# Attention scores of a streaming encoder: two matmuls of 128 and 64 rows per head become three of 64 rows, with two heads on two row groups in turn

## The chip, the cores and the metric

The kernel runs on one core of one Trainium2 chip. The metric is device time in microseconds, lower is better. Times are the median of several executions; the profile is one further execution, recorded by the hardware profiler, in which TensorE is called PE, its weight load PEld, VectorE DVE, ScalarE ACT, GpSimd POOL and the queue engine SP.

## The reference, cut to what matters

The program is one layer of a hybrid encoder: a gated linear recurrence (HGRN2) on half of the width, chunk-band attention on the other half, then an output product and a squared-ReLU MLP. It runs for a prompt of 2048 tokens and for eight streams of 16 tokens. Only the attention of the prompt is touched here. For each of 8 heads of width 64:

```
rel  = clip(kpos[None, :] - qpos[:, None], -128, 128) + 128
s    = q k^T * (1 / sqrt(64)) + rel_bias[:, rel]     # float32
s    = where(key in the chunk band, s, -1e30)
o    = softmax(s) v
```

A query of chunk c (64 tokens) reads the keys of the chunks c-8 to c. All inputs are float32, and the products are wanted at about float32 accuracy.

## The kernel before, in words

**Splitting for accuracy.** Nearly all products are made from matmuls of the type fp32r, which keeps fewer bits than fp32. So an operand x is kept as a high part, x rounded to fp32r, and a low part, the rest; a product is then hi·hi + hi·lo + lo·hi, three matmuls (`mm3`, lines 290 to 292). Weights are split while they stream in: ACT makes `whi` (line 256), DVE makes `wlo` (line 257).

**Stages.** Three stages follow one another: HGRN (up to about 783 us of the profile), attention (783 to 1484 us), MLP (from 1484 us). In the attention stage two streams of work are written out side by side by `weave`: `att_proj` (products for q, k, v of each group of up to three token tiles of 128, and the output product two groups behind), and `att` (the attention itself). The scheduler of the language then orders each engine's instructions; an engine runs its instructions strictly in that order. So the products of the first stream (`mm<-...`, 256 or 384 columns wide) are the filler that PE has while the softmax of a tile is worked on by DVE and ACT.

**One step of the attention** (`att_group`) is one token tile and one feature tile `ft`, that is, two heads e = 0 and 1: 16 tiles x 4 feature tiles, 64 steps. In each step:

1. PE makes the scores `S` of both heads (lines 679 and 680), 128 queries x up to 640 keys. With five key tiles (12 of the 16 token tiles) the 640 columns are made in two halves of 320; with fewer, in one piece of 128 to 512 columns. Each head has an `S` of two PSUM banks of its own.
2. DVE adds the bias and takes the minimum (`s<-S,bias`, line 688), ACT takes the exponential (`s<-s,m`, line 690), head by head.
3. PE transposes the probabilities of each head (`S<-ident,s`, line 699), back into the same PSUM; DVE copies one head's and ACT the other's to `pt` (line 700).
4. PE multiplies with v (`ps_oT<-pt,vt`, line 706). The two heads use 64 columns of the array each, in turn.

**The scores before.** Line 679 is a matmul over all 128 rows of the array: q's high part of head e stands twice, in the rows of e and in the other 64 rows (`q[:, e, :]`), and `K[:, e, :]` has k's high part in the rows of e and its low part in the other rows; so one matmul gives hi·hi + hi·lo. Line 680 adds lo·hi from 64 rows alone. Head e = 1 follows when e = 0 is complete:

```
nc.tensor.matmul(S[:, bk, :n], q[:, e, qc], c.K[ft][:, e, kc], start=True, stop=False)
nc.tensor.matmul(S[:, bk, :n], ql[es, qc], c.K[ft][es, e, kc], start=False, stop=True)
```

To lay the parts out in this way, `att_proj_group` takes for each feature tile of q four ACT instructions of 64 partitions (lines 881 and 885, once for each head) and two of DVE (line 882), and for each feature tile of k two of ACT (line 912) and two of DVE (line 913).

Of the kernel before, what the change touches and what calls it, by code (L numbers as in the profile page):

```python
# [8 lines left out]
F32 = mybir.dt.float32  # L9
F32R = mybir.dt.float32r  # L10
# [7 lines left out]
P = 128  # L18
D = 1024
KT = D // P  # L20
NPT = 16            # token tiles of the prompt; tile 16 holds the 8x16 sample tokens
NTT = 17
# [4 lines left out]
BIG = 1e30  # L27
WC = 256            # weight columns taken at a time

# [42 lines left out]
def rsq(c, ss, n, width, key="", r=None):  # L72
    """(ss / width + eps) ** -0.5 for a [P, n] tile of sums of squares"""
    nc = c.nc
    if r is None:
        r = c.small.tile([P, 8], F32, tag="r" + key, name="r", bufs=4)
    nc.gpsimd.tensor_scalar(out=r[:, :n], in0=ss, scalar1=1.0 / width, scalar2=EPS,
                            op0=ALU.mult, op1=ALU.add)
    nc.gpsimd.tensor_tensor(out=r[:, :n], in0=r[:, :n], in1=c.mhalf[:, :n], op=ALU.pow)
    return r  # L80
# [14 lines left out]
def transpose_split(c, src, hi, lo, col, nk=KT):  # L95
    """token rows src [P, nk*128] -> feature-major hi/lo parts [P, nk, col:col+128]"""
    nc = c.nc
    for k0 in range(0, nk, 4):
        ps = c.ps_tx.tile([P, 4, P], F32, tag=c.ps_tx_tag, name="tx")
        for k in range(4):  # L100
            nc.tensor.transpose(ps[:, k, :], src[:, (k0 + k) * P:(k0 + k + 1) * P], c.ident)  # L101
        h = hi[:, k0:k0 + 4, col:col + P]
        nc.scalar.copy(h, ps)
        nc.vector.tensor_tensor(out=lo[:, k0:k0 + 4, col:col + P], in0=ps, in1=h.bitcast(F32),  # L104
                                op=ALU.subtract)


def norm_rows(c, x, g, out, key=""):
    """out = x * rsqrt(mean(x^2) + eps) * g"""
    r = rsq(c, sumsq(c, x, D, key), 1, D, key)  # L110
    c.nc.vector.scalar_tensor_tensor(out=out, in0=x, scalar=r[:, 0:1], in1=g,
                                     op0=ALU.mult, op1=ALU.mult)


def weave(a, na, b, nb):
    """emit two streams of work side by side; a stream yields the share of work that it has emitted,
    or None while it waits for another"""
    done = [0.0, 0.0]
    live = [True, True]
    turn = None  # L120
    idle = 0
    while any(live):
        i = turn if turn is not None else int(done[0] * nb > done[1] * na)
        turn = None
        if not live[i]:
            i = 1 - i
        try:
            w = next((a, b)[i])
        except StopIteration:
            live[i] = False  # L130
            continue
        if w is None:
            turn = 1 - i
            idle += 1
            if idle > 1 or not live[1 - i]:
                yield None
                idle = 0
        else:
            done[i] += w
            idle = 0  # L140
            yield w
# [7 lines left out]
class HT:  # L149
    """normalised tokens of a group, feature-major, as hi/lo parts"""  # L150

# [7 lines left out]
    def pre(self, n=1):  # L159
        """loads of the next n token tiles"""  # L160
        while n and len(self.ld) < len(self.tiles) and self.ready():
# [3 lines left out]
    def add(self):  # L165
        """the next token tile"""
        j = self.next
# [37 lines left out]
def token_scale(c, t):  # L205
    """rsqrt of the mean square of the tokens of a tile, kept as a row of the scratch too"""
    nc = c.nc
# [7 lines left out]
class OT(HT):  # L215
    """mixer outputs of a group, feature-major, as hi/lo parts"""

# [24 lines left out]
class W:  # L242
    """a block [P, (nk, ncol)] of a weight matrix as hi/lo parts, in pieces"""

# [22 lines left out]
def wseq(c):  # L267
    """all blocks of weights in the order of their use, each prepared while the one before is in use"""
    srcs = [(c.w_in[i], WC) for _ in GROUPS for i in (4, 2, 3, 0, 1, 5, 6, 7)]
# [15 lines left out]
def mm3(c, ps, pairs, parts=1):  # L285
    """ps = sum of lhsT^T rhs over (lh, ll, rh, rl) parts, three passes each; yields between the parts"""
    nc = c.nc
# [13 lines left out]
def proj_fm(c, w, hT, n, parts=PARTS):  # L301
    """feature-major products, one PSUM tile after the other: yields (feature tile, columns, PSUM),
    before that as often as parts say without PSUM"""
    hi, lo = hT.hi, hT.lo
# [10 lines left out]
def proj_tm(c, w, hT, js, parts=PARTS):  # L315
    """token-major products: yields (token tile, PSUM) likewise"""
    hi, lo = hT.hi, hT.lo
# [15 lines left out]

# ---------------------------------------------------------------- HGRN

def lower_bound(c, pool):
    """lb = cumsum(softmax(lb_param, 0), 0) - softmax(lb_param, 0)[0], feature-major [P, 4]"""
    nc = c.nc
# [15 lines left out]
def hgrn_proj(c, gs, start):  # L354
    """projections of all groups, one after the other"""
    nc = c.nc
# [80 lines left out]
def hgrn_tile(c, g, j, t, seq):  # L437
    """one tile of 128 tokens: products of f between tokens, built up by doubling blocks"""
    nc = c.nc
# [122 lines left out]
def phase_hgrn(c):  # L562
    tc, nc = c.tc, c.nc
    with ExitStack() as s:
# [36 lines left out]
        def turn(act):  # L601
            """a level of each tile under way, until the first is done"""
            while True:
# [29 lines left out]

# ---------------------------------------------------------------- attention

def att_bias(c, h0, n):
    """negated bias of n heads, with the chunks that a row must not read"""
    nc = c.nc
# [7 lines left out]
def att_finish(c, o, t):  # L646
    """o [P, 512] token-major, normalised over its 512 features, to the scratch"""
    nc = c.nc
# [5 lines left out]
def att_group(c, g, tiles):  # L654
    """attention of a group's prompt tiles, one feature tile (two heads) after the other"""
    nc = c.nc
# [3 lines left out]
    for ft in range(4):  # L660
# [4 lines left out]
        for j, i in enumerate(tiles):  # L665
# [6 lines left out]
            st = []  # L672
            for e in range(2):
                h = 2 * ft + e
                es = slice(64 * e, 64 * e + 64)
                S = c.ps_s.tile([P, 2, 512], F32, tag="S", name="S")
                for (bk, o, n) in halves:
                    kc = slice(k0 + o, k0 + o + n)
                    nc.tensor.matmul(S[:, bk, :n], q[:, e, qc], c.K[ft][:, e, kc], start=True, stop=False)  # L679
                    nc.tensor.matmul(S[:, bk, :n], ql[es, qc], c.K[ft][es, e, kc], start=False, stop=True)  # L680
                s = c.sp.tile([P, 640], F32, tag="s", name="s")
# [45 lines left out]
def att_sample(c, qbd, kraw, vs):  # L727
    """8 streams x 16 queries over 256 cached and 16 new keys"""
    nc = c.nc
# [59 lines left out]
def att_proj(c, gs):  # L789
    """q, k, v of all groups and, two groups behind, w_out"""  # L790
    todo = TODO
# [19 lines left out]
def out_group(c, oT, nxt, pool=None):  # L811
    """x + [o_h, o_a] w_out, to the scratch"""
    nc = c.nc
# [26 lines left out]
def att_v(c, vt, tiles, hT):  # L840
    """the first half of v, by way of the tiles that hold all of it"""
    for t in tiles:
# [11 lines left out]
def att_proj_group(c, gs, gi, vt, hT, nxt):  # L854
# [13 lines left out]
    for ch in range(2):  # L868
        w = next(c.ws)
        for f, cs, ps in proj_fm(c, w, hT, n):  # L870
# [3 lines left out]
            ft = ch * 2 + f  # L874
            q = c.qp_.tile([P, 2, GMAX], F32R, tag="qd", name="qd")
            ql = c.qp_.tile([P, GMAX], F32R, tag="ql", name="ql")
            g.q[ft] = (q, ql)
            for e in range(2):
                src = slice(64 * e, 64 * e + 64)
                oth = slice(64 - 64 * e, 128 - 64 * e)  # L880
                nc.scalar.activation(q[src, e, :npr], ps[src, :npr], AF.Copy, scale=-0.125)
                nc.vector.scalar_tensor_tensor(
                    out=ql[src, :npr], in0=ps[src, :npr], scalar=-0.125,
                    in1=q.bitcast(F32)[src, e, :npr], op0=ALU.mult, op1=ALU.subtract)
                nc.scalar.activation(q[oth, e, :npr], ps[src, :npr], AF.Copy, scale=-0.125)
            if sample:
# [4 lines left out]
    for ch in range(2):  # L891
        w = next(c.ws)
        for f, cs, ps in proj_fm(c, w, hT, n):
# [14 lines left out]
            kc = slice(512, 512 + npr)  # L908
            for e in range(2):
                src = slice(64 * e, 64 * e + 64)  # L910
                oth = slice(64 - 64 * e, 128 - 64 * e)
                nc.scalar.copy(K[src, e, kc], raw[src, :npr])
                nc.vector.tensor_tensor(out=K[oth, e, kc], in0=raw[src, :npr],
                                        in1=K.bitcast(F32)[src, e, kc], op=ALU.subtract)
            fs = slice(ft * P, (ft + 1) * P)
# [59 lines left out]

# ---------------------------------------------------------------- MLP

# [22 lines left out]
def sample_mixer(c):  # L1000
    """attention and w_out of the sample tokens"""
    tc, nc = c.tc, c.nc
# [211 lines left out]
```

## Time and profile before

| | |
|---|---|
| median of 3 runs | 3121.32 us (3119.15 to 3126.25) |
| profiled execution, span from first to last instruction | 3136.9 us |
| PE busy | 2996.8 us (96%) |
| PE's weight loads | 2728.8 us (87%) |
| DVE busy | 1778.4 us (57%) |
| ACT busy | 1154.7 us (37%) |
| POOL busy | 302.5 us (10%) |
| DMA moved | 330.45 MB, mean 105 GB/s |

For the profiled execution nothing but its span is given, so the span stands for its time; it is 15.6 us longer than the median of the runs. Busy times of PE are modelled: a matmul's record covers its passage through the pipeline, so records that follow each other overlap, and what a matmul costs is read from the distance between the starts of two, not from the length of one.

### The profile page before, as it was taken

The numbers are of one execution on the slowest core, as the hardware profiler recorded it, in microseconds if no ns is written. First come the engines' busy times: TensorE is split into PE (matmuls) and PEld (weight loads), VectorE is DVE, ScalarE is ACT, GpSimd is POOL, SyncE is SP. The second block draws the span as 40 slices with busy tenths as digits, with TensorE's granted clock in tenths as the row PEclk, the third lists the DMA queues.
The fourth block names the chain that finished last, engine by engine and source line by source line (L and its number), as shares of the span: only waits on it lengthen the run. The fifth ranks groups of instructions, "written<-read, shape, count | busy, mean of one in ns | idle before, by whom it ended". The sixth has DMA issues, their size and how long they took to land.

```text
span 3136.9 us, 46880 instructions
## 1 busy us (share of the span) xinstructions
PE 2996.8 (96%) x18678; PEld 2728.8 (87%) x18678; DVE 1778.4 (57%) x3162; ACT 1154.7 (37%) x2354; POOL 302.5 (10%) x509
## 2 busy tenths in 40 slices
PE   5689999998999999999899999999999999999998
PEld 5678999998878888888888899999999999899997
DVE  3347566775546555565555545556555555655555
ACT  3332334344654545454422332323222222332332
POOL 2221222221002010100200000001000000000000
PEclk8789999999999999999999999999999999999999
DMA  8764233344315132333832232214221221422222
GB/s 156 154 123 130 92 124 111 105 136 135 109 55 165 64 127 84 130 127 123 287 101 81 83 111 93 88 61 155 68 68 60 67 67 56 147 70 79 81 71 71
DMA packets 118795, 330.45 MB, mean 105 GB/s; under 512 B 14192, under 2 KB 42480, under 8 KB 118576
## 3 DMA queue, kind: packets, MB, share of 16 engines
q1 hardware_dynamic: 111712, 308.84, 33.0%
q0 software_dynamic: 6864, 18.63, 1.5%
q8 instruction: 146, 2.39, 0.3%
q14 instruction: 73, 0.60, 0.1%
HBM read 294.90 MB, written 32.51 MB: 104 GB/s over the span
## 4 chain that ended last, share of the span: by engine, by line
PE 84%; DMA 8%; DVE 3%; issue 2%; POOL 2%; ACT 1%; SPq 0%; ACTq 0%; POOLq 0%; DVEq 0%
PE mm L290 23%; PE mm L292 23%; PE mm L291 23%; DMA x<-in_x_prompt 3%; PE ps_oT L706 2%; PE S L680 2%; PE S L679 2%; PE S L699 2%; PE ps_sc L472 2%; DMA wraw<-in_w_in 1%; DMA rd<-r 1%; DVE wlo L257 1%; DMA xT<-in_x_T 1%; PE tx L101 1%; PE ps_sc L465 1%
## 5 line engine op out<-in xcount | busy, mean ns | idle before, releaser
L256 ACT CAST whi<-wraw 128x512 fp32r<-128x512 f32 x816 | 498.0, 620 | 748.9 <-PE mm L292 550.4
L257 DVE TENSOR_TENSOR wlo<-wraw,whi 128x512 fp32r<-128x512 f32 x816 | 563.5, 707 | 245.0 <-ACT whi L256 241.1
L290 PE MATMUL mm<-h_hi,whi 128*128 128x384 f32 (+1 forms) x1536 | 503.6, 328 | 0.0
L292 PE MATMUL mm<-h_hi,wlo 128*128 128x384 f32 (+1 forms) x1536 | 502.0, 327 | 0.0
L291 PE MATMUL mm<-h_lo,whi 128*128 128x384 f32 (+1 forms) x1536 | 501.5, 326 | 0.0
L1087 DVE TENSOR_TENSOR y<-mm,y 128x512 f32<-128x512 f32 x544 | 373.7, 689 | 221.6 <-PE mm L292 219.9
L290 PE MATMUL mm<-whi,hT_hi 128*128 128x256 f32 x1264 | 385.7, 305 | 43.9 <-DVE gate L382 20.0
L292 PE MATMUL mm<-whi,ul 128*128 128x512 f32 x1088 | 424.1, 390 | 0.0
L291 PE MATMUL mm<-wlo,uh 128*128 128x512 f32 x1088 | 424.0, 390 | 0.0
L290 PE MATMUL mm<-whi,uh 128*128 128x512 f32 x1088 | 423.5, 389 | 0.0
L292 PE MATMUL mm<-whi,hT_lo 128*128 128x256 f32 x1264 | 375.5, 297 | 4.9 <-DVE hT_lo L104 3.5
L291 PE MATMUL mm<-wlo,hT_hi 128*128 128x256 f32 x1264 | 374.1, 296 | 0.0
L290 PEld LDWEIGHTS mm<-whi,hT_hi 128*128 128x128 f32 x1264 | 254.7, 202 | 56.0 <-DVE gate L382 21.2
L290 PEld LDWEIGHTS mm<-h_hi,whi 128*128 128x128 f32 x1536 | 289.0, 188 | 4.2 <-issue 2.6
L290 PE MATMUL mm<-hT_hi,whi 128*128 128x384 f32 (+1 forms) x768 | 266.3, 347 | 26.3 <-ACT sig L401 17.2
L291 PEld LDWEIGHTS mm<-h_lo,whi 128*128 128x128 f32 x1536 | 288.9, 188 | 1.2
L292 PEld LDWEIGHTS mm<-h_hi,wlo 128*128 128x128 f32 x1536 | 288.9, 188 | 0.0
L292 PEld LDWEIGHTS mm<-whi,hT_lo 128*128 128x128 f32 x1264 | 255.2, 202 | 9.8 <-DVE hT_lo L104 4.8
L1065 DVE SCALAR_TENSOR_TENSOR u<-mm,u 128x384 f32<-128x384 f32 (+1 forms) x192 | 102.5, 534 | 280.7 <-ACT u L1064 280.6
L291 PE MATMUL mm<-hT_lo,whi 128*128 128x384 f32 (+1 forms) x768 | 258.5, 337 | 0.0
L292 PE MATMUL mm<-hT_hi,wlo 128*128 128x384 f32 (+1 forms) x768 | 257.7, 336 | 0.0
L291 PEld LDWEIGHTS mm<-wlo,hT_hi 128*128 128x128 f32 x1264 | 255.3, 202 | 1.7 <-issue 1.4
(183 smaller groups left out, 4194.6 us busy)
## 6 DMA issues: line engine op xcount, KB each, us to landing
wraw<-in_w_in SPq DMA_DIRECT2D x168, 512.0 KB, 4.3
wraw<-in_w_up SPq DMA_DIRECT2D x96, 512.0 KB, 4.2
wraw<-in_w_down SPq DMA_DIRECT2D x96, 512.0 KB, 3.8
wraw<-in_w_out SPq DMA_DIRECT2D x48, 512.0 KB, 4.0
xT<-in_x_T SPq DMA_DIRECT2D x34, 512.0 KB, 4.5
og<-og SPq DMA_DIRECT2D x17, 512.0 KB, 3.7
x<-yo POOLq DMA_DIRECT2D x68, 128.0 KB, 3.7
x<-x SPq DMA_DIRECT2D x17, 512.0 KB, 5.1
```

The source lines that it names most:

```text
L256: nc.scalar.copy(hi, rw)
L257: nc.vector.tensor_tensor(out=lo, in0=rw, in1=hi.bitcast(F32), op=ALU.subtract)
L290: nc.tensor.matmul(ps, lh, rh, start=(i == 0), stop=False)
L291: nc.tensor.matmul(ps, lh, rl, start=False, stop=False)
L292: nc.tensor.matmul(ps, ll, rh, start=False, stop=(i == n - 1))
L472: nc.tensor.matmul(pc[:, h * n2:(h + 1) * n2, :], ks[:, h, :], up[:, h], start=True, stop=True)
L679: nc.tensor.matmul(S[:, bk, :n], q[:, e, qc], c.K[ft][:, e, kc], start=True, stop=False)
L680: nc.tensor.matmul(S[:, bk, :n], ql[es, qc], c.K[ft][es, e, kc], start=False, stop=True)
L699: nc.tensor.transpose(ps[:, x, :], s[:, x * P:(x + 1) * P], c.ident)
L706: nc.tensor.matmul(poT[64 * e:64 * e + 64, j, :], g.vt[i - nk + 1 + x][:, 64 * h:64 * h + 64], pts[e][:, x, :], start=(x == 0), stop=(x == ...
L1065: nc.vector.scalar_tensor_tensor(out=u2, in0=ps, scalar=0.0, in1=u2, op0=ALU.max, op1=ALU.mult)
L1087: nc.vector.tensor_tensor(out=ysl, in0=ps, in1=ysl, op=ALU.add)
```

## The change

The high and low parts of q and of k are kept in natural layout: partition p of `q`, `ql`, `K[:, 0]` and `K[:, 1]` is feature p of the two heads. Each head's scores are three matmuls over its own 64 rows: hi·hi, hi·lo, lo·hi. Both heads' `S` are allocated at the start of the step, and the matmuls of head 0 (rows 0 to 63) and head 1 (rows 64 to 127) alternate. Splitting q now takes one ACT and one DVE instruction of 128 partitions for a feature tile, splitting k one of each. The rest of the diff is comments that are gone, by which line numbers move.

```diff
@@ att_group
             st = []
-            for e in range(2):
+            Ss = [c.ps_s.tile([P, 2, 512], F32, tag="S", name="S") for _ in range(2)]
+            for (bk, o, n) in halves:
+                kc = slice(k0 + o, k0 + o + n)
+                for a, b in ((q, 0), (q, 1), (ql, 0)):
+                    for e, S in enumerate(Ss):
+                        es = slice(64 * e, 64 * e + 64)
+                        nc.tensor.matmul(S[:, bk, :n], a[es, qc], c.K[ft][es, b, kc],
+                                         start=(a is q and not b), stop=(a is ql))
+            for e, S in enumerate(Ss):
                 h = 2 * ft + e
-                es = slice(64 * e, 64 * e + 64)
-                S = c.ps_s.tile([P, 2, 512], F32, tag="S", name="S")
-                for (bk, o, n) in halves:
-                    kc = slice(k0 + o, k0 + o + n)
-                    nc.tensor.matmul(S[:, bk, :n], q[:, e, qc], c.K[ft][:, e, kc], start=True, stop=False)
-                    nc.tensor.matmul(S[:, bk, :n], ql[es, qc], c.K[ft][es, e, kc], start=False, stop=True)
                 s = c.sp.tile([P, 640], F32, tag="s", name="s")
@@ att_proj_group
-            q = c.qp_.tile([P, 2, GMAX], F32R, tag="qd", name="qd")
+            q = c.qp_.tile([P, GMAX], F32R, tag="qd", name="qd")
             ql = c.qp_.tile([P, GMAX], F32R, tag="ql", name="ql")
             g.q[ft] = (q, ql)
-            for e in range(2):
-                src = slice(64 * e, 64 * e + 64)
-                oth = slice(64 - 64 * e, 128 - 64 * e)
-                nc.scalar.activation(q[src, e, :npr], ps[src, :npr], AF.Copy, scale=-0.125)
-                nc.vector.scalar_tensor_tensor(
-                    out=ql[src, :npr], in0=ps[src, :npr], scalar=-0.125,
-                    in1=q.bitcast(F32)[src, e, :npr], op0=ALU.mult, op1=ALU.subtract)
-                nc.scalar.activation(q[oth, e, :npr], ps[src, :npr], AF.Copy, scale=-0.125)
+            nc.scalar.activation(q[:, :npr], ps[:, :npr], AF.Copy, scale=-0.125)
+            nc.vector.scalar_tensor_tensor(out=ql[:, :npr], in0=ps[:, :npr], scalar=-0.125,
+                                           in1=q.bitcast(F32)[:, :npr], op0=ALU.mult, op1=ALU.subtract)
@@ att_proj_group
-            for e in range(2):
-                src = slice(64 * e, 64 * e + 64)
-                oth = slice(64 - 64 * e, 128 - 64 * e)
-                nc.scalar.copy(K[src, e, kc], raw[src, :npr])
-                nc.vector.tensor_tensor(out=K[oth, e, kc], in0=raw[src, :npr],
-                                        in1=K.bitcast(F32)[src, e, kc], op=ALU.subtract)
+            nc.scalar.copy(K[:, 0, kc], raw[:, :npr])
+            nc.vector.tensor_tensor(out=K[:, 1, kc], in0=raw[:, :npr], in1=K.bitcast(F32)[:, 0, kc],
+                                    op=ALU.subtract)
```

**First place: PE, the scores of token tile 5 in feature tile 2.** The rows are the matmuls in PE's order, with the stationary part last; the last pair of numbers is 128 queries x columns. `S_10219` and `S_10228` are the scores of heads 0 and 1, `qd` and `ql` the high and low part of q. Before, with the first product of the filler behind them:

```order
L679 MATMUL S_10219<-K012_6929,qd_8530 128x320
L680 MATMUL S_10219<-K012_6929,ql_8531 128x320
L679 MATMUL S_10219<-K012_6929,qd_8530 128x320
L680 MATMUL S_10219<-K012_6929,ql_8531 128x320
L679 MATMUL S_10228<-K012_6929,qd_8530 128x320
L680 MATMUL S_10228<-K012_6929,ql_8531 128x320
L679 MATMUL S_10228<-K012_6929,qd_8530 128x320
L680 MATMUL S_10228<-K012_6929,ql_8531 128x320
L290 MATMUL mm_10194<-hT_hi_102,whi_10044 128x384
```

Eight matmuls, of 128 and 64 rows in turn, first all of head 0. In the change the same place reads as follows, with `S_10211` and `S_10212` as the two heads:

```order
L679 MATMUL S_10211<-K012_6929,qd_8498 128x320
L679 MATMUL S_10212<-K012_6929,qd_8498 128x320
L679 MATMUL S_10211<-K012_6929,qd_8498 128x320
L679 MATMUL S_10212<-K012_6929,qd_8498 128x320
L679 MATMUL S_10211<-K012_6929,ql_8499 128x320
L679 MATMUL S_10212<-K012_6929,ql_8499 128x320
L679 MATMUL S_10211<-K012_6929,qd_8498 128x320
L679 MATMUL S_10212<-K012_6929,qd_8498 128x320
L679 MATMUL S_10211<-K012_6929,qd_8498 128x320
L679 MATMUL S_10212<-K012_6929,qd_8498 128x320
L679 MATMUL S_10211<-K012_6929,ql_8499 128x320
L679 MATMUL S_10212<-K012_6929,ql_8499 128x320
```

Twelve matmuls, all of 64 rows, with the heads in turn, so that head 0 is complete one matmul before head 1. Between these and the first transposes stand 12 products of 384 columns, before and in the change. Of the 64 steps the scheduler leaves most in one piece: in PE's whole order the matmuls of the scores form 77 unbroken runs before and 81 in the change.

**Second place: PE, from the last score matmul of token tile 3 in feature tile 2 to the first transposes.** This is one of the places with the least filler; the last row is the transposes of head 0. Before:

```order
L680 MATMUL S_8875<-K012_6929,ql_7686 128x512
L291 MATMUL mm_8951<-hT_lo_103,whi_8627 128x384
L292 MATMUL mm_8951<-hT_hi_102,wlo_8628 128x384
L290 MATMUL mm_8951<-hT_hi_102,whi_8633 128x384
L291 MATMUL mm_8951<-hT_lo_103,whi_8633 128x384
L292 MATMUL mm_8951<-hT_hi_102,wlo_8634 128x384
L290 MATMUL mm_8951<-hT_hi_102,whi_8633 128x384
L291 MATMUL mm_8951<-hT_lo_103,whi_8633 128x384
L292 MATMUL mm_8951<-hT_hi_102,wlo_8634 128x384
L290 MATMUL mm_8951<-hT_hi_102,whi_8637 128x384
L291 MATMUL mm_8951<-hT_lo_103,whi_8637 128x384
L699 MATMUL S_8868<-ident_63,s_8871 128x128 x4
```

In the change, where the transposes have line 701:

```order
L679 MATMUL S_8835<-K012_6929,ql_7658 128x512
L292 MATMUL mm_8921<-hT_hi_102,wlo_8590 128x384
L290 MATMUL mm_8921<-hT_hi_102,whi_8595 128x384
L291 MATMUL mm_8921<-hT_lo_103,whi_8595 128x384
L292 MATMUL mm_8921<-hT_hi_102,wlo_8596 128x384
L290 MATMUL mm_8921<-hT_hi_102,whi_8595 128x384
L291 MATMUL mm_8921<-hT_lo_103,whi_8595 128x384
L292 MATMUL mm_8921<-hT_hi_102,wlo_8596 128x384
L290 MATMUL mm_8921<-hT_hi_102,whi_8599 128x384
L291 MATMUL mm_8921<-hT_lo_103,whi_8599 128x384
L701 MATMUL S_8834<-ident_63,s_8842 128x128 x4
```

The filler went from ten products to nine. One product and then the four transposes of head 1 follow in both.

**Third place: ACT, one q of the first group.** Before, the four instructions for one q stand among exponentials and weight casts:

```order
L881 ACTIVATE qd_7610<-mm_7585 64x384
L690 ACTIVATE s_7662,rs_7569<-s_7662,m_7663 128x256
L690 ACTIVATE s_7669,rs_7569<-s_7669,m_7670 128x256
L885 ACTIVATE qd_7610<-mm_7585 64x384
L881 ACTIVATE qd_7610<-mm_7585 64x384
L700 COPY pt_7697<-S_7666 128x256
L885 ACTIVATE qd_7610<-mm_7585 64x384
```

In the change:

```order
L702 COPY pt_7591<-S_7544 128x128
L880 ACTIVATE qd_7584<-mm_7559 128x384
L692 ACTIVATE s_7637,rs_7541<-s_7637,m_7638 128x256
L692 ACTIVATE s_7641,rs_7541<-s_7641,m_7642 128x256
L702 COPY pt_7665<-S_7630 128x256
```

One instruction of 128 partitions stands where four of 64 stood, and the PSUM tile `mm` is read by fewer instructions.

## Rows read from the trace of the kernel before

**Rows 1.** Page of the profile: busy us, share of the span, instructions.

```profile
PE 2996.8 (96%) x18678; PEld 2728.8 (87%) x18678; DVE 1778.4 (57%) x3162; ACT 1154.7 (37%) x2354; POOL 302.5 (10%) x509
```

**Rows 2.** Attention stage: us, busy PE, PEld, DVE, ACT, POOL, clock, DMA share, GB/s.

```profile
783.00:1484.00 701.00, 693.44 (x4866) 589.29 (x4866) 388.71 (x738) 361.39 (x746) 60.79 (x96) 0.98 0.34 109
```

**Rows 3.** Waits, 783 to 1484 us: total, times, longest; L679's row reads alike.

```profile
PEld S L680 <- issue: 33.2, 205, 0.3
```

**Rows 4.** Timeline of PE, 999.8 to 1007.8 us: start, duration, line, shape.

```profile
999.89 0.41 PE L679 MATMUL S<-K,qd 128*128 128x320 f32 x1
1000.23 0.41 PE L680 MATMUL S<-K,ql 64*128 64x320 f32 x1
1000.57 0.38 PE L290 MATMUL mm<-whi,hT_hi 128*128 128x256 f32 x1
1000.79 0.28 PE L291 MATMUL mm<-wlo,hT_hi 128*128 128x256 f32 x1
1000.91 0.28 PE L292 MATMUL mm<-whi,hT_lo 128*128 128x256 f32 x1
...
1002.10 0.71 PE L699 MATMUL S<-ident,s 128*128 128x128 f32 x5
...
1002.77 0.71 PE L699 MATMUL S<-ident,s 128*128 128x128 f32 x5
...
1006.15 1.31 PE L706 MATMUL ps_oT<-pt,vt 128*64 128x128 f32 x20
1007.39 0.41 PE L679 MATMUL S<-K,qd 128*128 128x320 f32 x1
```

**Rows 5.** Timeline of PE near 858 and 913 us: scores and products of other widths.

```profile
857.52 0.50 PE L679 MATMUL S<-K,qd 128*128 128x512 f32 x1
857.95 0.50 PE L680 MATMUL S<-K,ql 64*128 64x512 f32 x1
...
913.52 0.34 PE L290 MATMUL mm<-hT_hi,whi 128*128 128x384 f32 x1
913.70 0.34 PE L291 MATMUL mm<-hT_lo,whi 128*128 128x384 f32 x1
```

**Rows 6.** Timeline of PE, short stretches that begin at column tiles' first matmuls.

```profile
1006.15 0.33 PE L706 MATMUL ps_oT<-pt,vt 128*64 128x128 f32 x2
...
1731.90 0.44 PE L743 MATMUL S<-kT,qbd 128*32 128x272 f32 x4
1731.90 0.67 PE L743 MATMUL S<-kT,qbd 128*32 128x272 f32 x8
```

**Rows 7.** Timeline of DVE and ACT behind the scores that end at 1000.57 us.

```profile
1000.68 0.82 DVE L688 CUSTOM_DVE_ANT_0 s<-S,bias 128x640 f32<-128x640 f32 x1 [0.53 <-PE S L680]
1001.43 0.08 DVE L688 DVE_READ_ACCUMULATOR2_ANT m<- 128x1 f32 x1
1001.61 0.83 ACT L690 ACTIVATE s<-s,m 128x640 f32<-128x640 f32 x1 [0.50 <-DVE m L688]
```

**Rows 8.** Busy time by stretch, the nine of low granted clock in the attention stage.

```profile
897.67:901.08 3.41, 3.41 (x14) 3.24 (x14) 1.63 (x5) 2.46 (x6) 0.00 (x0) 0.50 0.14 53
...
1464.28:1467.69 3.41, 3.41 (x18) 3.41 (x18) 0.74 (x3) 1.12 (x4) 0.00 (x0) 0.50 0.13 38
sum 34.11, PE 34.11 PEld 33.11 DVE 17.71 ACT 18.58 POOL 1.92; mean PE 3.79 PEld 3.68 DVE 1.97 ACT 2.06 POOL 0.21
```

**Rows 9.** Timeline of PE, around the last of these falls.

```profile
1463.88 0.39 PE L290 MATMUL mm<-whi,hT_hi 128*128 128x256 f32 x1
...
1464.59 0.42 PE L291 MATMUL mm<-wlo,hT_hi 128*128 128x256 f32 x1
1464.81 0.41 PE L292 MATMUL mm<-whi,hT_lo 128*128 128x256 f32 x1
```

**Rows 10.** Groups of instructions, 783 to 1484 us: splitting q; L885, L912 alike.

```profile
L881 ACT ACTIVATE qd<-mm 64x384 fp32r<-64x384 f32 (+1 forms) x40 | 18.6, 464 | 20.8 <-PE S L679 11.9 <-PE mm L292 8.6
L882 DVE SCALAR_TENSOR_TENSOR ql<-mm,qd 64x384 fp32r<-64x384 f32 (+1 forms) x40 | 21.1, 527 | 19.8 <-ACT qd L881 19.4
```

## The prediction

> **What bounds the kernel now.** I read the page's busy times first: PE is busy for 2996.8 of 3136.9 us, DVE for 57%, ACT for 37% [rows 1]. Then the stage that the change touches: from 783 to 1484 us PE is busy for 693.4 of 701.0 us, DVE for 389, ACT for 361, and the DMA engines for about a third [rows 2]. So in this stage time is PE's, and the rest follows it. Last, what a score matmul costs, from the distance between starts in PE's timeline. Scores of 320 columns start 0.34 us apart (999.89, 1000.23, 1000.57), while products of 256 columns start 0.12 apart (1000.79, 1000.91) [rows 4] and those of 384 columns 0.18 [rows 5]; 320 should take about 0.147. The reader is to see that 0.2 us of each 0.34 is not streaming. The waits name it: the weight load of line 680 stood idle 205 times for 33.2 us in all, for "issue", so for nothing outside PE, and that of line 679 alike [rows 3]. What is peculiar to these places is that 128 rows and 64 rows alternate. The entry to the scores from `ps_oT` (64 columns) and the return from 64 rows to 128 cost the same 0.2: the last score at 1000.23 has its follower at 1000.57, the one after that at 1000.79 [rows 4].
>
> **The score blocks.** At 512 columns the distance is 0.43 (857.52 to 857.95) [rows 5]. Against 0.34 at 320 that is 0.09 for 192 columns; so I take 0.365 for 384, 0.31 for 256 and 0.26 for 128. A step with five key tiles costs 8 x 0.34 = 2.72 us now, and there are 12 x 4 = 48 of them; each narrower width has 4 steps of 4 matmuls. All score blocks together: 48 x 2.72 + 4 x 4 x (0.43 + 0.365 + 0.31 + 0.26) = 152 us.
>
> The change has 12 matmuls in place of 8, but none changes the number of rows. What remains unknown is whether the two row groups run side by side; no row of before shows two row groups in turn. The nearest rows show column groups: two `ps_oT` matmuls of different column halves end as a pair within 0.33, 20 of them take 1.31 us (0.11 a pair), and four of line 743, with 32 columns each, take 0.44 together, and eight 0.67; a second round of four adds only 0.23 [rows 6]. So parts of the array with operands of their own do work at once, and their weight loads don't queue visibly. I take that for row groups too: a pair costs one matmul at full pace. A block of 320 is then 5 x 0.147, plus 0.01 for the partner, plus 0.34 for the last pair and the return to 128 rows: 1.085 us. It saves 1.635 us, 48 times: 78.5. Narrow blocks have three pairs: at 512, 2 x 0.228 + 0.44 = 0.90 in place of 1.72; likewise 0.72 for 1.46, 0.56 for 1.24, 0.49 for 1.04; 2.8 a set, 11 for four sets. **Together -89.6.**
>
> The bounds: if each pair were two matmuls in file, a block would be 11 x 0.147 + 0.34 = 1.96; if every matmul still cost 0.34, 4.08. Both are rivals below.
>
> A rule bears on this. The Trainium skill, "TensorEngine Tiling (Array Packing)", Key Properties, says that changing the tiling mode, but not just the tile, drains the engine, and that different tiles can load and multiply in parallel. The 0.34 in place of 0.147 at each change between 128 and 64 rows agrees [rows 4]; for tiles of one mode only the column groups speak here [rows 6]. By the rule the sum is the one just made; by the 0.34 alone it would be a loss.
>
> **Broken blocks.** In PE's order 81 runs of score matmuls stand for 64 steps. Each of the 17 extra breaks now costs about 0.34 - 0.147 at its end and some 0.2 on the way back in, where before the switch was paid in any case: **+6**.
>
> **The new wait.** Before, head 0 was complete four matmuls (1.36 us) before head 1; now both end together, so DVE's pass over head 1 queues behind that of head 0. From the start of the last score matmul (1000.23) DVE starts 0.45 later, ACT's exponential 0.93 after that, and the transposes 1.16 after the exponential's start (1001.61 to 1002.77) [rows 4, 7]: 2.54 us. Head 1's come one DVE pass (0.82) later, at 3.36. The filler begins 0.34 after the last score. At token tile 5 in feature tile 2, with 12 products of 0.174, PE reaches head 0's transposes at 0.34 + 2.09 = 2.43 and waits 0.11; after five transposes of 0.11 it is at 3.09 and waits 0.27 more. At token tile 3 in feature tile 2 there are nine products: 0.34 + 1.57 = 1.91, and with shorter passes at 512 columns the two waits come to about 0.45. Where 24 products of 0.12 stand between, nothing waits. Going through the order in this way, 28 of 64 steps wait, 8 us in all. Behind a waiting transpose stand the filler, the copies to `pt` and the products with v; a late exponential or a weight cast ahead of it on DVE or ACT adds some: **+10**.
>
> **The clock.** Nine stretches of the attention stage, 34.1 us in all, run at the granted clock 0.50, the 1.2 GHz level, instead of 2.4 [rows 8]; in the last of them products start 0.22 apart instead of 0.12 [rows 9]. In eight of the nine a whole score block (in the last it returns to the products at 1463.88) ends within 0.7 us before the fall, and in the ninth part of a block does. So the drained blocks bring them about. At half speed 34 us hold 17 us of lost time. With blocks of 1.1 us in place of 2.7 I expect most to go: **-14**, between 0 and -17.
>
> **Splitting q and k.** ACT loses three of four instructions of 0.46 for each q and one of two for k, DVE one of two of 0.53 for each [rows 10]. They lie under PE's work: 45 us of ACT and 25 us of DVE over the program, on engines busy for 52% and 55% of the stage. I take nothing; PE's idle time in the stage, 7.6 us [rows 2], is the most it could give back. The copies of older keys (line 907) are unchanged. No DMA is added or moved.
>
> **Sum.** -89.6 + 6 + 10 - 14 = -87.6. The profiled span 3136.9 becomes 3049.3; it stands 15.6 us above the median of the runs, and I take the same difference off: 3121.3 - 87.6 = **3034 us**. HGRN and MLP stay as they are. A change within 0.2% (6 us) could not be told from none.
>
> **Rivals.**
> *Pairs run at once, but their weights don't.* Two loads of 128 columns in file would set the pace; transposes, with a load each, start (0.71 - 0.28)/4 = 0.11 apart [rows 4], so a pair would cost 0.22. A block of 320 is 1.45, the gain on blocks 70, the time **3054**. The Trainium skill, "TensorE: Matmul & The Clock Gate", Part 3, says that a load overlaps matmuls in flight only when the row group differs. Here a head's next load would then wait for its own matmul, 0.11 + 0.13 = 0.24 a pair, and the time would be 3059. Against it: from 256 to 384 columns the distance grows by about 0.055, so 256 columns stream for 0.11, and products 0.12 apart leave no room for an unhidden load, with equal rows [rows 4, 5]. Chance 0.13, taken at 3056.
> *In file, without drains.* Twelve at 0.147: the gain on blocks is 40, the time **3083**. Against it speak the column groups; chance 0.10.
> *A drain at each change of row group* (the slower case). Twelve at 0.34 are 4.08 us, +1.36 for 48 blocks and +11 for the narrow ones: +76 in place of -89.6, and no relief of the clock; with the +10 for the waits, **3207**. It turns into a loss when matmuls stand over 0.227 apart (2.72/12). For it: fp32r at 64 rows never ran here without a switch beside it. Chance 0.08.
> *Half arrays count as idle for the clock.* If each of 64 blocks brought a low stretch of 3.4 us like those now, they would cost 109 us instead of 17: -89.6 + 6 + 10 + 92 = +18, **3140**. Against it: the low stretches follow blocks in which PE stands empty for 0.2 of each 0.34 us, and these pairs leave no such gaps; chance 0.05.
>
> **How the numbers follow.** The main case has 0.64, by itself 3014 to 3052 (clock and waits at their ends, and narrow blocks off by a little). With the first two rivals the range is 3014 to 3088, which leaves out about 0.17. Faster: 0.64 + 0.13 + 0.10 = 0.87. Slower: 0.08 and most of the last 0.05, 0.11. Same: 0.02.
>
> **What will show it.** Starts of the first and second score matmul some 0.01 apart and pairs 0.147 apart in PE's timeline: right; equal distances of 0.147 or 0.34 name the rival. Weight loads that wait for "issue" at scores should fall from 66 us to a few. Waits of line 701 for ACT should appear, some 8 to 10 us. The stage should end near 1396 instead of 1484, with few low stretches. It is wrong if score blocks of 320 take over 1.5 us, if transposes wait for over 25 us, or if the clock in the stage falls below 0.98.

## The result: 3034 us, 2.8% faster, and the profile after

The changed kernel takes 3034.24 us in the median of 4 runs (3027.65 to 3037.46), the kernel before 3120.24 beside it (3115.58 to 3126.25): ratio 0.9715, 95% interval 0.9697 to 0.9734. Two further series of the same kernel gave 0.9734 (0.9715 to 0.9754) and 0.9730 (0.9712 to 0.9747). The prediction was 3034, ratio 0.972.

The page's busy times, which answer to [rows 1]:

```profile
PE 2904.2 (96%) x18902; PEld 2680.0 (88%) x18902; DVE 1746.6 (58%) x3114; ACT 1103.7 (36%) x2258; POOL 301.5 (10%) x509
```

PE has 224 matmuls more (18902 against 18678) and is busy 93 us less. ACT lost 51 us, DVE 32.

The attention stage by itself, from the start of the first score matmul to that of the last (columns as in [rows 2]); first the kernel before, then the change:

```profile
783.07:1476.03 692.96, 685.40 (x4795) 581.54 (x4794) 384.72 (x731) 358.85 (x741) 60.18 (x95) 0.98 0.34 109
```

```profile
765.30:1373.70 608.40, 597.81 (x5017) 539.78 (x5018) 355.34 (x689) 314.70 (x661) 60.97 (x95) 1.00 0.38 123
```

The stage is 84.6 us shorter, and its granted clock is 1.00 where it was 0.98. The profiled span fell by 104 us, from 3136.9 to 3032.8, because the profiled execution of before had also lost some 18 us in its HGRN stage, which the change does not touch: its first score starts at 783.1, and in the twelve other profiles of this study at 763 to 770. So the fall of the stage, not that of the span, is to be compared with the 86.0 us that the runs gained.

One score block of five key tiles (all score matmuls of a step, up to the next product), in PE's timeline. First an unbroken block of before, with its first and last rows, as [rows 4] has no whole one:

```profile
1437.28 0.41 PE L679 MATMUL S<-K,qd 128*128 128x320 f32 x1
...
1439.66 0.41 PE L680 MATMUL S<-K,ql 64*128 64x320 f32 x1
1440.00 0.39 PE L290 MATMUL mm<-whi,hT_hi 128*128 128x256 f32 x1
```

Then the change. A row merges matmuls that overlap or touch; the last number is how many:

```profile
844.07 0.56 PE L679 MATMUL S<-K,qd 64*128 64x320 f32 x4
844.47 0.31 PE L679 MATMUL S<-K,ql 64*128 64x320 f32 x2
844.62 0.46 PE L679 MATMUL S<-K,qd 64*128 64x320 f32 x4
844.91 0.31 PE L679 MATMUL S<-K,ql 64*128 64x320 f32 x2
845.15 0.44 PE L290 MATMUL mm<-hT_hi,whi 128*128 128x384 f32 x1
```

From the first score at 844.07 to the next product at 845.15 it is 1.08 us, as forecast (1.085), where the kernel before needs 2.72 (1437.28 to 1440.00). These two are typical: the medians over the unbroken blocks of five key tiles are 2.72 us (39 blocks) and 1.07 us (36 blocks). A row of two `ql` lasts as long as one matmul does: the starts of a pair are 0.003 us apart, the second pair starts 0.25 behind the first, the others follow at 0.146, and from the last pair to the product it is 0.236.

PE's waits of the stage (total us, times, longest), which answer to [rows 3]:

```profile
PEld S L679 <- issue: 12.8, 73, 0.3
PEld S L701 <- ACT s L692: 10.7, 26, 1.9
```

The 66 us that weight loads of scores stood idle for "issue" have become 13, and the transposes of line 701 now wait 10.7 us for exponentials.

### The profile page after: what moved, and what is told of

The parts are those of the page before. It is cut to its first block, busy times and chain, and to the rows that moved or that the text cites. A ratio compares the mean times of both kernels' runs of the same rounds, so it can differ in the third digit from the quotient of the medians.

```text
span 3032.8 us, 47202 instructions
## 1 busy us (share of the span) xinstructions
PE 2904.2 (96%) x18902; PEld 2680.0 (88%) x18902; DVE 1746.6 (58%) x3114; ACT 1103.7 (36%) x2258; POOL 301.5 (10%) x509
## 4 chain that ended last, share of the span: by engine, by line
PE 81%; DMA 8%; DVE 4%; ACT 2%; issue 2%; POOL 2%; SPq 0%; ACTq 0%; POOLq 0%; DVEq 0%
PE mm L290 23%; PE mm L292 23%; PE mm L291 23%; PE ps_oT L708 3%; DMA x<-in_x_prompt 2%; PE S L679 2%; PE S L701 2%; PE ps_sc L472 2%; DMA wraw<-in_w_in 1%; DMA rd<-r 1%; ACT junk L87 1%; DVE wlo L257 1%; PE ps_sc L465 1%; PE tx L101 1%; DMA x<-x 1%
```

## The experiments

Each is given by its edit, what was on record before it ran, and what came of it. Ratios are to the kernel before, on the same chip.

**Head after head.** All score matmuls of head 0, then all of head 1:

```diff
-            for (bk, o, n) in halves:
-                kc = slice(k0 + o, k0 + o + n)
-                for a, b in ((q, 0), (q, 1), (ql, 0)):
-                    for e, S in enumerate(Ss):
-                        es = slice(64 * e, 64 * e + 64)
+            for e, S in enumerate(Ss):
+                es = slice(64 * e, 64 * e + 64)
+                for (bk, o, n) in halves:
+                    kc = slice(k0 + o, k0 + o + n)
+                    for a, b in ((q, 0), (q, 1), (ql, 0)):
```

> The change with one edit: all score matmuls of head 0, then all of head 1, so that the row group changes once in a step and not at every matmul. Theory (row groups in turn run side by side, a pair costs one matmul): a block of 320 columns grows from 1.08 to 1.08 + 6 x 0.147 = 1.96 us, 48 times, +42, and the narrow ones by +4; head 0 is complete six matmuls sooner, which gives back about 5 us of waiting transposes: 3034 + 41 = 3075 us, ratio to the kernel before 0.985. Rival (the whole gain is the switch between 128 and 64 rows that is gone, and the order of heads does nothing): 3034, ratio 0.972.

Measured: 3062.17 us, ratio 0.9827 (0.9810 to 0.9843). The direction is that of the theory, the size is not: +28 us by the medians, +35 by the ratios, where 41 was expected, and half of the blocks' +0.88 us was missing (1.48 us instead of 1.96). The blocks fell short of the forecast by 23 us (48 x 0.48), the time by 13 or 6: 20.5 us of the stage run at the low clock in this profile, which costs 10 us, and in that of the change none do. PE's timeline of one block says why the blocks are shorter:

```profile
845.77 0.56 PE L679 MATMUL S<-K,qd 64*128 64x320 f32 x2
846.17 0.31 PE L679 MATMUL S<-K,ql 64*128 64x320 f32 x1
846.18 0.59 PE L679 MATMUL S<-K,qd 64*128 64x320 f32 x4
846.57 0.34 PE L679 MATMUL S<-K,ql 64*128 64x320 f32 x2
846.72 0.45 PE L679 MATMUL S<-K,qd 64*128 64x320 f32 x2
847.01 0.31 PE L679 MATMUL S<-K,ql 64*128 64x320 f32 x1
847.25 0.44 PE L290 MATMUL mm<-hT_hi,whi 128*128 128x384 f32 x1
```

In PE's order of instructions each head has two `qd`, one `ql`, two `qd`, one `ql`, and head 1 follows head 0. Run in that order, the sequence would be 2, 1, 2, 1, 2, 1, 2, 1. The trace shows 2, 1, **4, 2**, 2, 1: the first half of head 1 runs together with the second half of head 0, from 7 ns after head 0's third matmul on. So PE started matmuls of the other row group ahead of three older ones, and three matmuls' time was saved. The rows do not name the head; that the early ones are head 1's is read from the counts and from the starts, which form two trains, each with 0.25 us to its second matmul and 0.147 from there on. It also limits what was said of the kernel before, that an engine runs its instructions strictly in order: here PE did not. This experiment therefore did not take the second row group away; the one with one row group, below, does.

**Grouped.** The kernel before with its eight matmuls sorted by kind (both heads' `S` are then allocated at the start of the step, as in the change; cut to the matmuls):

```diff
-            for e in range(2):
-                ...
-                    nc.tensor.matmul(S[:, bk, :n], q[:, e, qc], c.K[ft][:, e, kc], start=True, stop=False)
-                    nc.tensor.matmul(S[:, bk, :n], ql[es, qc], c.K[ft][es, e, kc], start=False, stop=True)
+            Ss = [c.ps_s.tile([P, 2, 512], F32, tag="S", name="S") for _ in range(2)]
+            for (bk, o, n) in halves:
+                ...
+                for e, S in enumerate(Ss):
+                    nc.tensor.matmul(S[:, bk, :n], q[:, e, qc], c.K[ft][:, e, kc], start=True, stop=False)
+            for (bk, o, n) in halves:
+                ...
+                for e, S in enumerate(Ss):
+                    ...
+                    nc.tensor.matmul(S[:, bk, :n], ql[es, qc], c.K[ft][es, e, kc], start=False, stop=True)
```

> The kernel before, its layout and splitting kept, with the eight score matmuls of a step in another order: the four of 128 rows first, then the four of 64 rows with the two heads in turn. Theory (what cost was the switch between 128 and 64 rows, once for each matmul): one switch in a block instead of eight, 4 x 0.147 + 0.2 for the switch, two pairs, and the return: about 1.3 us where the change has 1.08 and the kernel before 2.72; 3034 + 0.2 x 64 = 3047 us, ratio 0.976. Rival (the natural layout or the shorter splitting brings the gain): 3121, ratio 1.0.

Measured: 3052.96 us, ratio 0.9798 (0.9781 to 0.9814). A block in PE's timeline:

```profile
847.70 0.85 PE L677 MATMUL S<-K,qd 128*128 128x320 f32 x4
848.48 0.56 PE L682 MATMUL S<-K,ql 64*128 64x320 f32 x4
848.97 0.45 PE L290 MATMUL mm<-hT_hi,whi 128*128 128x384 f32 x1
```

1.27 us for the same eight matmuls that took 2.72: another order alone, with layout and splitting as they were, brings 2.0% of the 2.7 to 2.85%. The rival (layout or splitting) is out as the main cause. The order does two things at once: it leaves one of the seven switches inside a block, and it puts the four matmuls of 64 rows on two row groups in pairs (the four of 848.48 take the time of two). The next experiment has the first without the second. By the median this kernel is 6 us slower than expected, by the ratio 12; the longer splitting, which it keeps, is worth 8 (below), and 13.7 us of its stage run at the low clock.

**All 128 rows.** The low part of q stands twice as well:

```diff
-                    nc.tensor.matmul(S[:, bk, :n], ql[es, qc], c.K[ft][es, e, kc], start=False, stop=True)
+                    nc.tensor.matmul(S[:, bk, :n], ql[:, e, qc], c.K[ft][:, e, kc], start=False, stop=True)
...
-            ql = c.qp_.tile([P, GMAX], F32R, tag="ql", name="ql")
+            ql = c.qp_.tile([P, 2, GMAX], F32R, tag="ql", name="ql")
...
-                nc.vector.scalar_tensor_tensor(
-                    out=ql[src, :npr], in0=ps[src, :npr], scalar=-0.125,
-                    in1=q.bitcast(F32)[src, e, :npr], op0=ALU.mult, op1=ALU.subtract)
+                for d in (src, oth):
+                    nc.vector.scalar_tensor_tensor(
+                        out=ql[d, e, :npr], in0=ps[src, :npr], scalar=-0.125,
+                        in1=q.bitcast(F32)[src, e, :npr], op0=ALU.mult, op1=ALU.subtract)
...
-        c.qp_ = pool("a_q", 5)
+        c.qp_ = pool("a_q", 4)
```

> The kernel before with the low part of q standing twice as well, so that its second score matmul has 128 rows too (it adds lo times lo, which neither kernel has): eight matmuls of 128 rows, none of 64, no two row groups, four buffers for q and its low part instead of five for room, and one more DVE instruction for each head and q. Theory (switches are what cost): 8 x 0.147 = 1.18 us to the next product, 0.1 more than the change, 48 times, +5; head 0 complete four matmuls sooner, -3; entries from products need no switch, -1: 3035 us, ratio 0.973. Rival (the gain needs two row groups side by side): 3080 or more, ratio 0.987 or more.

Measured: 3055.93 us, ratio 0.9806 (0.9793 to 0.9820). A block, first and last rows, in PE's timeline:

```profile
849.06 0.41 PE L678 MATMUL S<-K,qd 128*128 128x320 f32 x1
849.31 0.31 PE L679 MATMUL S<-K,ql 128*128 128x320 f32 x1
849.46 0.31 PE L678 MATMUL S<-K,qd 128*128 128x320 f32 x1
...
850.19 0.31 PE L679 MATMUL S<-K,ql 128*128 128x320 f32 x1
850.34 0.34 PE L290 MATMUL mm<-hT_hi,whi 128*128 128x384 f32 x1
```

Eight matmuls, the second 0.25 behind the first and the others 0.147 apart, 1.28 us in all: with the switches gone and no second row group, a block of before loses 1.44 us, so two row groups are not needed for most of the gain. The rival (3080 or more) is out. The kernel came out 21 us (by the ratio 24) slower than expected. The blocks are 0.1 longer than the 1.18 expected, by the first distance, which is 5 us over 48 of them. In its trace PE also stands at group boundaries and at transposes (one distance between `ps_oT` and a product is 3.4 us), and 20.5 us of the stage run at the low clock, which costs 10 us. Which of its three side changes (DVE's additional instructions, the longer splitting, four buffers) costs most was not separated.

**Splitting as before.** The change, with q and k split by as many instructions of 64 partitions as before:

```diff
-            nc.scalar.activation(q[:, :npr], ps[:, :npr], AF.Copy, scale=-0.125)
-            nc.vector.scalar_tensor_tensor(out=ql[:, :npr], in0=ps[:, :npr], scalar=-0.125,
-                                           in1=q.bitcast(F32)[:, :npr], op0=ALU.mult, op1=ALU.subtract)
+            for e in range(2):
+                src = slice(64 * e, 64 * e + 64)
+                for _ in range(2):
+                    nc.scalar.activation(q[src, :npr], ps[src, :npr], AF.Copy, scale=-0.125)
+                nc.vector.scalar_tensor_tensor(out=ql[src, :npr], in0=ps[src, :npr], scalar=-0.125,
+                                               in1=q.bitcast(F32)[src, :npr], op0=ALU.mult, op1=ALU.subtract)
...
-            nc.scalar.copy(K[:, 0, kc], raw[:, :npr])
-            nc.vector.tensor_tensor(out=K[:, 1, kc], in0=raw[:, :npr], in1=K.bitcast(F32)[:, 0, kc],
-                                    op=ALU.subtract)
+            for e in range(2):
+                src = slice(64 * e, 64 * e + 64)
+                nc.scalar.copy(K[src, 0, kc], raw[src, :npr])
+                nc.vector.tensor_tensor(out=K[src, 1, kc], in0=raw[src, :npr], in1=K.bitcast(F32)[src, 0, kc],
+                                        op=ALU.subtract)
```

> The change with q and k split by as many instructions as before: for each q four of ACT and two of DVE, for each k two and two, each of 64 partitions. Theory (they lie under PE's work): 3034 us within 0.2%, ratio 0.972, with ACT's busy time up by about 45 us and DVE's by 25. Rival (shorter splitting frees PSUM and starts scores sooner, a part of the gain): 3040 to 3050, ratio 0.975 to 0.978.

Measured: 3048.17 us, ratio 0.9779 (0.9765 to 0.9793): not within 0.2% of the change, but in the range of the rival. No time of the change was taken beside it there, so the two were measured side by side.

> The change itself, once more, beside the kernels of this call, so that they can be compared on one chip: ratio to the kernel before 0.9715 within 0.002, score blocks of 320 columns 1.08 us.

> The change with the splitting of q and k in as many instructions of 64 partitions as before, again, now beside the change. Theory (the splitting is worth something: more ACT and DVE instructions ahead of the exponentials make the transposes wait longer, 17 us instead of 11 in the traces, and the clock falls behind such waits): ratio 0.004 to 0.007 above that of the change, 12 to 22 us. Rival (the difference between the two calls was the chip): the same ratio as the change within 0.002.

Measured: the change 3037.05 us (3032.75 to 3040.34), ratio 0.9734 (0.9715 to 0.9754); the version with the longer splitting 3044.84 (3043.16 to 3047.88), ratio 0.9764 (0.9745 to 0.9784). The ratios' intervals overlap, but no run of the one falls among those of the other: 8 us, less than the 12 to 22 expected.

**ACT's part alone.** The same edit for ACT's instructions only:

```diff
-            nc.scalar.activation(q[:, :npr], ps[:, :npr], AF.Copy, scale=-0.125)
+            for e in range(2):
+                src = slice(64 * e, 64 * e + 64)
+                for _ in range(2):
+                    nc.scalar.activation(q[src, :npr], ps[src, :npr], AF.Copy, scale=-0.125)
...
-            nc.scalar.copy(K[:, 0, kc], raw[:, :npr])
+            for e in range(2):
+                src = slice(64 * e, 64 * e + 64)
+                nc.scalar.copy(K[src, 0, kc], raw[src, :npr])
```

> The change with only ACT's part of the splitting as before (four instructions for a q, two for a k), DVE's part as in the change. Theory (ACT's instructions stand ahead of exponentials): most of the difference between the change and its version with both parts, ratio 0.003 to 0.006 above the change. Rival (DVE's part does it, by way of its passes over the scores): the ratio of the change within 0.002.

Measured: 3048.02 us (3040.55 to 3051.11), ratio 0.9770 (0.9748 to 0.9792), 11 us over the change. The waits of transposes for exponentials in the stage (total us, times, longest), for the change, for both parts, and for ACT's part:

```profile
PEld S L701 <- ACT s L692: 12.4, 28, 2.0
```

```profile
PEld S L701 <- ACT s L692: 18.3, 35, 2.6
```

```profile
PEld S L701 <- ACT s L692: 20.3, 36, 4.6
```

Six to eight us more of the one wait that the change introduced: ACT's additional instructions stand in its queue ahead of exponentials. DVE's part is not needed for it. What the rival of the longer splitting named, scores that start later, is small: weight loads of scores wait 1.6 us for ACT's splitting of k in the version with both parts.

**One row group.** Both heads on rows 0 to 63, in the order of the change:

```diff
-                        es = slice(64 * e, 64 * e + 64)
+                        es = slice(0, 64)
                         nc.tensor.matmul(S[:, bk, :n], a[es, qc], c.K[ft][es, b, kc],
```

> The change with both heads' matmuls on rows 0 to 63 (head 1's scores are made from head 0's q and k), in the same order. Nothing but the second row group is gone. Theory (a pair costs one matmul because two row groups run side by side): twelve in file, 11 x 0.147 + 0.1 + 0.236 = 1.95 us for a block of 320 where the change has 1.08; 48 x 0.87 + 4 = +46 us, ratio 0.986 to 0.987. Rival (64-row matmuls of one group overlap as well): ratio as the change.

Measured: 3072.33 us, ratio 0.9851 (0.9828 to 0.9873), 35 us over the change on the same chip. A block in PE's timeline:

```profile
848.18 0.85 PE L679 MATMUL S<-K,qd 64*128 64x320 f32 x4
848.87 0.45 PE L679 MATMUL S<-K,ql 64*128 64x320 f32 x2
849.16 0.75 PE L679 MATMUL S<-K,qd 64*128 64x320 f32 x4
849.75 0.45 PE L679 MATMUL S<-K,ql 64*128 64x320 f32 x2
850.13 0.45 PE L290 MATMUL mm<-hT_hi,whi 128*128 128x384 f32 x1
```

848.18 to 850.13 is 1.95 us, as expected: twelve in file, the second 0.25 behind the first, the others at 0.147, and 0.236 to the product. Over the stage the distances from each score matmul to PE's next matmul add up to 116 us, against 73 in the change: +43 for +46 expected. The time grew by less than the blocks, 35 us. The rest came back at the transposes: the distances from another matmul to a transpose sum to 16.1 us instead of 21.6, those between transposes to 52.0 instead of 54.3, and the transposes' weight loads wait 4.6 us for exponentials instead of 12.4. That the longer blocks leave DVE and ACT time for what stands ahead of the softmax in their queues is a guess.

**More filler ahead of the transposes.** The remaining wait, attacked by the shares of the other stream:

```diff
-Y1, Y2 = 1.7, 1.7
+Y1, Y2 = 2.3, 1.2
```

> The change itself beside the two kernels of this call: ratio 0.9725 within 0.002.

> The change with the shares of the filler moved: Y1, Y2 = 2.3, 1.2 in place of 1.7, 1.7, so that more products stand between scores and transposes and fewer between transposes and the products with v. Theory (the transposes' wait for exponentials is what is left of the change's cost): by the order of instructions and the durations of the trace 8 us of waits in place of 11, so 3 us less, within 0.2% of the change and not to be told from it; waits of line 701 for ACT down from 12 to about 9 us. Rival (the products with v then wait for the copies instead): the same or a few us more.

> The same with Y1, Y2 = 2.6, 0.9: by order and durations 6 us of waits in place of 11, the copies behind the transposes 1 us worse; 4 us less than the change at best, ratio 0.001 below it; waits of line 701 for ACT at 6 us. Rival: the wait moves to the products with v, no gain.

Measured: the change 3038.28 us, ratio 0.9730 (0.9712 to 0.9747); 2.3 and 1.2 gave 3037.32, 0.9734 (0.9716 to 0.9752); 2.6 and 0.9 gave 3036.29, 0.9728 (0.9712 to 0.9745). The wait for exponentials fell from 12.6 to 10.2 and 8.9 us, and the products with v now wait 5.3 and 6.8 us for the copies instead of 3.8: the wait moves more than it goes, and no version can be told from the change.

## Why the prediction was right, and which of its terms were off

**The score blocks: right, by the mechanism given.** Forecast -89.6 with +6 for broken blocks, -83.6; measured, as the sum of distances behind score matmuls in the stage, 155.1 us before and 73.5 after, -81.6. Both halves of the mechanism were shown apart. Taking away the alternation of 128 and 64 rows, with as many matmuls and no second row group, brings a block from 2.72 to 1.28 us (all 128 rows). Taking away only the second row group brings it from 1.08 to 1.95. So of the 1.64 us of a block 0.77 is that the switches are gone, though twelve matmuls stand in file for eight (2.72 to 1.95), and 0.87 is that a pair costs one. That the block came out at 1.08 to the hundredth is luck, as two errors cancelled: the second pair starts 0.25 behind the first, not 0.147, and the return to 128 rows costs 0.236 in place of 0.34. The rule quoted from the Trainium skill, "TensorEngine Tiling (Array Packing)", Key Properties, is borne out: 0.2 at each change of the number of rows, none at a change of row group (the grouped block shows the 0.2 in its two parts: 0.234 to the first matmul behind the change and 0.25 to the next, in place of 0.147 each).

**The rivals: refuted.** Pairs follow each other at 0.146, not at the 0.22 or 0.24 of exposed weight loads. With one row group alone, twelve matmuls follow each other at 0.147, so a load is hidden behind matmuls of its own rows. The Trainium skill, "TensorE: Matmul & The Clock Gate", Part 3, says that it overlaps only where the row group differs; here the measurement decides against that sentence. With one row group the load is hidden down to 256 columns (starts 0.118 apart near 775.53); at 128 columns they are 0.112 apart (near 766.29), as transposes are 0.11, where the wider ones would lead one to expect about 0.06 (an estimate from 0.174 at 384 and 0.118 at 256), so there something else sets the pace, perhaps the load. The drain at each change of row group (3207 us) and the pairs in file (3083 us) are refuted by starts 0.003 us apart, and the half arrays that count as idle for the clock (3140 us) by the stage's clock of 1.00.

**The new wait: right.** +10 was forecast; weight loads of transposes waited 10.7 us for exponentials in the first profile and 12.4 and 12.6 in two more, against 1.4 for line 699 before. In distances between starts it is +6.2 us into transposes and +2.8 between them.

**The clock: right in kind, at the far end in size.** Nine low stretches of 34.1 us became none between the first and the last score, so -17 by the working of the prediction where -14 was taken; two more profiles of the change had 0 and 3.4 us. The granted clock of whole runs agrees, as an estimate: its median is 0.979 before and 0.984 with the change in one later series, 0.977 and 0.981 in the other, which comes to 17 and 14 us. Two kinds of fall are to be told apart. Before, seven of the nine falls come behind a whole score block, with no two starts over 0.35 us apart just before. In the other twelve profiles, which have no such alternation, 17 of 18 falls come right behind or within a distance of about 1.3 us or more between two starts (0.85 in the other). The kernel with one row group has blocks of 1.95 us without gaps and no fall in the stage. So it is drained blocks, and not long ones, that go with the first kind; that they cause it is argued from these counts, and was not tested by itself. The drains are not the whole account, either: grouped and all 128 rows have one switch or none inside a block, and yet 13.7 and 20.5 us of low clock in the stage, and their whole runs have a median of 0.9805 and 0.980, like the 0.980 of before beside them. Grouped has no more distances of 1 us or more in the stage than the change (four against five), so why its clock fell and that of the change hardly did stays open.

**Splitting: the term that was mis-sized.** "I take nothing" was wrong by 8 us of 3037, and the bound beside it, PE's 7.6 us of idle time before, does not hold for a wait that only the change brings. The cover that I named, PE's work, hides ACT's additional instructions only where no exponential is queued behind them; since the change made the transposes wait for exponentials, ACT's queue is on the path there. The error did not show in the total, which is luck: with the splitting as before the wait is 18 us, so the +10 came true only because the splitting became shorter.

**What is left over.** With half of each low stretch counted as lost, the distances between PE's starts split the stage's -84.6 in full: score blocks -80.7 (the 0.8 to 81.6 lies in the low clock), the clock -17.1, transposes +6.2 and +2.8, and everything else +4.3. The last is spread over many small distances, the largest +2.0 among the products and +1.3 from `ps_oT` to scores (six more such entries, from blocks broken in the order), and was not pinned down. Against the forecast the blocks gained 3 us less and the clock 3 more, the transposes cost 1 less, and 4 came from where none was forecast; so the near total, -87.6 for the runs' -86.0, owes something to luck.

## What to carry to other kernels

Read a matmul's cost from the distance between starts, and look for places where matmuls over 128 and over 64 rows alternate: here each cost 0.34 us where 0.147 was streaming, and another order of the same matmuls already gave 2%. Two independent products over 64 rows each belong on different row groups side by side; here that paid even at the price of half as many matmuls again. Where two halves now end together, their consumers queue; so every instruction ahead of those consumers on ACT and DVE then has a price that it did not have before.

## What the runs showed of the hardware that was not expected

Matmuls of another row group started ahead of older ones in PE's order: head 1's first matmul 7 ns after head 0's third, with three of head 0 still to start, and the block took 1.48 us instead of 1.95. The first distance behind a change of tiling (the rows and columns of the array that a matmul uses) is 0.25 us at 320 columns instead of 0.147, whichever way the change goes: after `ps_oT` for 64 rows (844.07) as for 128 rows (849.06 to 849.31).
